# One Trainium2 core, a hybrid S5 and short-convolution layer with sixteen experts: everything up to the experts in a hand order

## The chip, the cores and the metric

The kernel runs on one core of one Trainium2 chip. The metric is the device time of one execution in microseconds (us), the median of the runs. The engines are TensorE (PE; its weight loads are PEld), VectorE (DVE), ScalarE (ACT), GpSimd (POOL) and SyncE (SP); SP issues most transfers, and each engine works through its own list in order.

## What is computed

x is (512, 1024), ctx (256, 1024), all in fp32. The reference, cut to what matters:

```python
mx = ada_mod(c, w_mod, b_mod)              # six vectors of 1024: silu(c) @ w_mod + b_mod
hx = modulate(x, norm1_g, mx[0], mx[1])    # rmsnorm(x, g) * (1 + scale) + shift
hc = modulate(ctx, norm1_g, mc[0], mc[1])  # mc: the same of c_ctx
zx = hx @ w_in                             # 256 columns for the S5 part, 3 x 768 for the convolution
y_s5 = s5_readout(...)                     # two diagonal complex scans, forward and backward, then GELU and a gate
y_conv = short_conv_latent(zx[..., 256:], conv_w)   # b * conv3(c * v), along rows and along columns
x = x + mx[2] * (concat(y_s5, y_conv) @ w_out)
h = modulate(x, norm2_g, mx[3], mx[4])     # routing: best of 4 groups, best 2 of its 4 experts
x = x + mx[5] * hier_moe(h, ...)           # 16 experts: (silu(h @ w1) * (h @ w3)) @ w2
return rmsnorm(x, final_g)
```

## The kernel before

Large products run in a split form: `split` (L75) writes an operand as a high part (a copy on ACT, L74) and a low part (a subtraction on DVE), and `mm3` (L97) multiplies high by high, low by high and high by low, so eight chunks of 128 make 24 matmuls of 128x512. Small products are plain fp32 (`mm`, L91), transposes L195.

The stages, in the order of the program:

- Modulation, first part: the first 2048 columns of w_mod come in 16 loads of 512 KB, [128, 8, 128] with runs of 512 B (L124, `load_mod`), each used by eight matmuls of 2 output rows (L91, 128*2). x and ctx come in, get normed row by row (L501 to L503, the Newton steps of `rsqrt` on DVE in L203 to L213), are transposed and scaled.
- u, the input projection of the S5 part (48 matmuls for x, 48 of half width for ctx).
- Tables of the S5 part: powers, input and output matrices, phasors W. Their complex products (`cmul`, L310 to L315: six elementwise instructions each) run on DVE (`MinT`, 128x1024) and on POOL (W, and the output matrices CA, 128x576).
- 18 conv blocks, six times c, v and b, each of 24 matmuls with a 512 KB piece of w_in; beside them the drive (L91, 128*64 128x96: two column halves of PE in alternation), the inside products (128*32 128x128: one group of 32 columns), the scans (L638 to L667) and the other 4096 columns of w_mod (`mod_rows`). These are summed up per row chunk by DVE (L735), or by ACT (L739) with POOL (L740), and then spread over the partitions by a matmul with ones_f.
- w_out: 16 pieces of 12 matmuls. POOL multiplies each piece by mx2 (L869), then it is split.
- Routing: logits (L937), the norm's factor rs, the choice by one-hot tables, a one-hot gather of expert 0's tokens by matmuls (X0, with the tables OH), the slot table and the indices idx. The modulated rows go to DRAM (td), from where POOL's indirect transfers gather the tokens of experts 1 to 15 (L1024). `columns(e)` transposes them (L195).
- 16 experts of up to 96 tokens each. Their weights come in pieces of 512 KB through a ring of 34 buffers; from piece 34 on a load waits for the load six pieces earlier.

Up to the experts a scheduler orders the instructions of each engine; the generators' calls (`run(cv_, 1)`, `run(mods_, 2)`) only say in which order it sees them. The experts are in an order written by hand (`tc.manual_schedule`), with SP left to the scheduler.

## Time and profile before

| | us |
|---|---|
| median of 3 runs (684.26 to 691.06) | 684.47 |
| the profiled execution | 688.22 |
| its span (first to last instruction) | 686.5 |
| PE busy in the span | 595.4 |
| DVE busy | 538.8 |
| ACT busy | 357.0 |
| POOL busy | 276.5 |

The span is the time from the first to the last recorded instruction of the profiled execution; 1.7 us of the execution lie around it. Busy time is what an engine's instructions take; matmuls are pipelined, so a busy PE can still wait inside for its weights. The granted clock (PEclk) is the share of TensorE's full clock that the chip let it have. A releaser, written behind an arrow, is what ended an engine's idle time.

### The profile page before, as it was taken

To read this page: it belongs to the slowest core of one execution; us is meant where nothing else is said; L and a number is where in the kernel's file an instruction comes from. 1 tells how busy PE (TensorE), PEld (TensorE's weight loads), DVE (VectorE), ACT (ScalarE), POOL (GpSimd) and SP (SyncE) were. 2 spreads that over 40 slices of the span, in tenths; PEclk is the share of its full clock that TensorE was granted. 3 is DMA by queue.
4 is the path that set the end of the run, shared out by engine and by line. 5 is a ranking of instruction groups with operands and counts; after the bars stand their busy time and mean duration, and the time that the engine had idled before them with its cause. 6 is when DMAs were issued, how large, how long until landed. Compare 5 with 4: busy or idle time off the path is not lost.

```text
span 686.5 us, 9226 instructions
## 1 busy us (share of the span) xinstructions
PE 595.4 (87%) x3002; PEld 441.8 (64%) x3003; DVE 538.8 (78%) x813; ACT 357.0 (52%) x498; POOL 276.5 (40%) x233
## 2 busy tenths in 40 slices
PE   6776839899787798999979999999999999999970
...
PEclk9797788899898799998968999999999999999996
...
GB/s 185 217 258 222 2 31 42 201 219 214 154 169 209 134 244 178 224 238 191 354 275 273 326 363 355 362 364 366 365 366 363 365 360 359 359 352 374 133 146 125
DMA packets 111091, 172.26 MB, mean 251 GB/s; under 512 B 14219, under 2 KB 51431, under 8 KB 111039
## 3 DMA queue, kind: packets, MB, share of 16 engines
...
## 4 chain that ended last, share of the span: by engine, by line
DMA 32%; issue 24%; DVE 18%; PE 16%; SPq 3%; ACT 3%; POOL 3%; POOLq 0%; DVEq 0%; ACTq 0%
DMA b<-td,idx 12%; PE bank L97 10%; DMA b<-in_w_mod_dram 7%; PE bank L91 4%; DMA yd<-b,idx 4%; DVE b L75 4%; DMA b<-in_w_in_dram 2%; DVE b L735 2%; DMA b<-in_expert_w_dram 1%; SPq L120 1%; ACT b L74 1%; DMA b<-in_norm_g_dram 1%; PE bank L195 1%; DMA b<-in_ctx_dram 1%; DMA b<-yd 1%
## 5 line engine op out<-in xcount | busy, mean ns | idle before, releaser
L97 PE MATMUL bank<-b,b 128*96 128x512 f32 (+2 forms) x1872 | 458.9, 402 | 22.3 <-DVE b L75 10.8
L97 PEld LDWEIGHTS bank<-b,b 128*96 128x96 f32 (+1 forms) x1872 | 322.4, 177 | 136.7 <-DVE b L75 14.7
L75 DVE TENSOR_TENSOR b<-b,b 128x1024 fp32r<-128x1024 f32 (+2 forms) x249 | 291.3, 1214 | 48.4 <-ACT b L74 46.1
L74 ACT ACTIVATE b<-b 128x1024 fp32r<-128x1024 f32 (+3 forms) x254 | 240.4, 980 | 77.4 <-POOL b L869 23.8
L1024 POOL DMA_INDIRECT b<-td,idx x15 | 18.8, 1255 | 194.5 <-PE bank L195 141.3
L1029 POOL DMA_INDIRECT yd<-b,idx x15 | 69.0, 4600 | 39.1 <-DVE b L1123 38.7
L195 PE MATMUL bank<-ident,b 96*128 96x96 f32 (+4 forms) x343 | 48.6, 279 | 24.9 <-ACT b L503 10.4
L195 PEld LDWEIGHTS bank<-ident,b 96*128 96x128 f32 (+4 forms) x343 | 41.0, 156 | 36.4 <-ACT b L503 10.7
L735 DVE SCALAR_TENSOR_TENSOR b<-b,sc,b 128x512 f32<-128x512 f32 x36 | 32.4, 899 | 25.9 <-DMA b<-in_w_mod_dram 16.8
L740 POOL TENSOR_TENSOR b<-b,b 128x512 f32<-128x512 f32 x21 | 30.8, 1468 | 47.7 <-ACT b L739 36.5
L74 ACT ACTIVATE b<-bank 128x384 fp32r<-128x384 f32 x46 | 22.0, 479 | 37.6 <-PE bank L195 37.6
L91 PE MATMUL bank<-b,sc 128*2 128x128 f32 x256 | 35.2, 302 | 7.1 <-DMA b<-in_w_mod_dram 6.7
L91 PE MATMUL bank<-b,b 128*64 128x96 f32 (+5 forms) x320 | 35.6, 289 | 6.4 <-DVE b L465 5.0
L869 POOL TENSOR_TENSOR b<-b,b 128x512 f32<-128x512 f32 x16 | 22.6, 1416 | 45.5 <-DMA b<-in_w_out_dram 33.3
L91 PEld LDWEIGHTS bank<-b,b 128*64 128x64 f32 (+3 forms) x312 | 27.5, 150 | 14.8 <-POOL b L740 5.4
L739 ACT ACTIVATE b<-b,sc 128x512 f32<-128x512 f32 x21 | 15.2, 723 | 38.2 <-DMA b<-in_w_mod_dram 38.2
L91 PEld LDWEIGHTS bank<-b,sc 128*2 128x2 f32 x256 | 22.8, 93 | 18.2 <-DMA b<-in_w_mod_dram 9.0
L75 DVE TENSOR_TENSOR b<-bank,b 128x384 fp32r<-128x384 f32 x46 | 25.3, 551 | 4.0 <-ACT b L74 3.9
L1123 DVE SCALAR_TENSOR_TENSOR b<-bank,gate,b 96x512 f32<-96x512 f32 x32 | 22.5, 739 | 1.3 <-PE bank L97 1.3
L501 ACT ACTIVATE b<-b 128x1024 f32<-128x1024 f32 x6 | 6.3, 1054 | 31.0 <-DMA b<-in_x_dram 23.7
L310 POOL TENSOR_TENSOR b<-b 128x16 f32<-128x16 f32 (+4 forms) x12 | 5.5, 455 | 30.7 <-DVE Asc L252 29.8
L503 ACT ACTIVATE b<-b,ss 128x1024 f32<-128x1024 f32 x6 | 6.9, 1149 | 20.2 <-DVE ss L213 19.0
...
## 6 DMA issues: line engine op xcount, KB each, us to landing
b<-in_expert_w_dram SPq DMA_DIRECT2D x192, 512.0 KB
...
```

The lines of the kernel that those rows point to most:

```text
L74: S.activation(hi, x_, AF.Copy)
L75: return (e or V).tensor_sub(lo, x_, f32(hi))
L91: T.matmul(o, l, r, start=start, stop=stop)
L97: T.matmul(o, l, r, start=start and n == 0, stop=stop and n == 2)
L195: T.transpose(o, i, ident[0:n, 0:n])
L735: V.scalar_tensor_tensor(acc[q], m[:, kk], sc[:, k:k + 1], acc[q], op0=OP.mult, op1=OP.add)
L739: S.activation(m[:, kk], m[:, kk], AF.Copy, scale=sc[:, k:k + 1])
L740: P.tensor_add(acc2, acc2, m[:, kk])
L869: P.tensor_mul(wor[i], wor[i], mx2[h])
L1024: return P.indirect_dma_start(out=xg, out_offset=None, in_=td[:, :], in_offset=bass.IndirectOffsetOnAxis(ap=idx[:, e:e + 1], axis=0), boun ...
L1029: P.indirect_dma_start(out=yd[:, :], out_offset=bass.IndirectOffsetOnAxis(ap=ix, axis=0), in_=src, in_offset=None, bounds_check=639, oob_i ...
L1123: V.scalar_tensor_tensor(yt[:, r], yb[h][0:CAP], gate[:, e:e + 1], mx5[h][0:CAP], op0=OP.mult, op1=OP.mult)
```

## The change

Everything before the experts is put into the hand order too, SP's list included: one `tc.manual_schedule` around the whole program. The 18 conv blocks become a loop of steps: split the weights of block i + 1, multiply block i, one unit of `mod_rows`, evict block i - 1, at most one piece of the S5 part for PE (`task`), and so much DVE work of the S5 part as fits a share of 5.0, 3.0 or 4.5 us by costs that the generators state (`spend`).

Beside the order the change alters work:

- w_mod's first part comes as [2, 512] pieces with runs of 2 KB, multiplied by 32 matmuls of 32 output columns by 512 in four column groups of PE, and a small matmul with `sel` adds the groups. B and C of the S5 part are loaded as they lie, in runs of 4 KB, and turned by PE.
- `mod_rows` is computed on PE: 16 units of four matmuls 32x512 in four column groups, a bias matmul ahead of every second, and `sel` in place of ones_f. Its sums on DVE, ACT and POOL go.
- The S5 tables W and CA are computed on DVE instead of POOL, in the loop.
- w_out: the first half is multiplied by mx2 after the product, the second half on DVE instead of POOL; six buffers; the S5 blocks come last.
- Routing: XA = XR * A2 on POOL; X0 is gathered from XR, scaled afterwards; the td rows, gates, tables, slots and counts come later, and gather(1) follows the slots beside expert 0; 40 instead of 22 warm-up matmuls.
- w1 and w3 pieces are loaded with runs of 4 KB (four rows to a partition), and the chunks of the tokens are taken with a stride of four (`chunk`). Loads wait for the one six earlier from piece 22 on; 20 pieces are requested before the td stores.

The diff, cut to its core:

```diff
+    order_ = tc.manual_schedule(engines={mybir.EngineType.PE, mybir.EngineType.DVE, mybir.EngineType.Activation,
+                                         mybir.EngineType.Pool, mybir.EngineType.SP})
+    order_.__enter__()
...
     def load_mod(q):
-        m = (q // 4 % 2) * 8 + q // 8 * 4 + q % 4
-        D.dma_start(wm_slot[q % 8], dap(w_mod, m * 128, [[6144, 128], [6144 * 128, 8], [1, 128]]))
+
+        D.dma_start(wm_slot[q % 8], dap(w_mod, q % 8 * 128 * 6144 + q // 8 * 512, [[6144, 128], [1024, 2], [1, 512]]))
...
+    def mod_pair(half, kp):
+
+        if kp == 0:
+            mb[:] = [nb("v"), nb("v")]
         for s in range(2):
...
-            cmul(P, W[:, 0, :, n + 1:n + m], W[:, 1, :, n + 1:n + m],
...
+            cmul(V, W[:, 0, :, n:n + m], W[:, 1, :, n:n + m], W[:, 0, :, 1:m + 1], W[:, 1, :, 1:m + 1],
...
+    def row_unit(u):
+
+        q, k4 = u // 2, u % 2
+        if k4 == 0:
+            rowb[0] = nb("m")
+            mm(rowb[0][0:32], ones_f[0:1, 0:32], acc[q][0:1], True, False)
+        for k in range(4 * k4, 4 * k4 + 4):
+            mm(rowb[0][group(k)], sc[:, k:k + 1].to_broadcast([128, 32]), mslot[k // 2 % 2][:, k % 2], 0 < k < 4, k >= 4)
+        row_loads(u + 1)
+
...
+        b = nb("m")
+        mm(b, sel[:, 0:1].to_broadcast([128, 128]), acc[q], True, True)
...
-                    if kk == 0 or q == 7:
-                        V.scalar_tensor_tensor(acc[q], m[:, kk], sc[:, k:k + 1], acc[q], op0=OP.mult, op1=OP.add)
-                    elif k2 == 0:
-                        S.activation(acc2, m[:, kk], AF.Copy, scale=sc[:, k:k + 1])
-                    else:
-                        S.activation(m[:, kk], m[:, kk], AF.Copy, scale=sc[:, k:k + 1])
-                        P.tensor_add(acc2, acc2, m[:, kk])
...
-            mm(b, ones_f, acc[q], True, True)
...
+        for u in range(16):
+            if u % 2 == 0 and u:
+                row_wide(u // 2 - 1)
+            row_unit(u)
+            if u % 2:
+                row_sum(u // 2)
+            yield
+        row_wide(7)
+        yield
...
+        return slice(q // 4 * 512 + q % 4, q // 4 * 512 + 512, 4)
...
-    w13 = [[(src[0, e, k2 * 256:(k2 + 1) * 256].rearrange("(k p) f -> p k f", p=128), [2, 512])
-            for src in (expert_w1, expert_w3) for k2 in range(4)] for e in range(16)] + [[]]
+    w13 = [[(src[0, e, k2 // 2 * 512:(k2 // 2 + 1) * 512].rearrange("(p j) f -> p j f", j=4)
+             [:, k2 % 2 * 2:k2 % 2 * 2 + 2], [2, 512]) for src in (expert_w1, expert_w3) for k2 in range(4)] for e in range(16)] + [[]]
...
-            if n_load[0] >= len(ring):
+            if n_load[0] >= 22:
                 after(d, loads[n_load[0] - 6], "few loads in flight")
...
+        if h == 1:
+            V.tensor_mul(wor[i], wor[i], mx2[h])
+        split(wor[i], woh[i], wol[i])
...
+    beside = in_turn(marked("in0", s5_input(0)), marked("in1", s5_input(1)), s5_phasors(), s5_output(0),
+                     marked("bb0", s5_inside(0)), s5_output(1), marked("bb1", s5_inside(1)),
+                     s5_scan(0), marked("scan", s5_scan(1)))
+
+    def spend(us):
+        while us > 0:
+            c_ = next(beside, None)
+            if c_ is None:
+                return
+            us -= c_
+
+    tasks = [("in0", lambda: s5_input_turned(0)), ("in1", lambda: s5_input_turned(1)),
+             (None, lambda: s5_drive(0)), (None, lambda: s5_drive(1)),
+             ("bb0", lambda: s5_inside_mm(0)), ("bb1", lambda: s5_inside_mm(1)),
+             ("scan", lambda: (s5_rows(0), s5_rows(1))), (None, s5_gelu), (None, s5_gelu_turned), (None, s5_glu)]
+
+    def task(ready):
+        if tasks and (tasks[0][0] is None or tasks[0][0] in ready):
...
+    for i in range(1, 18):
+        ready = set(done)
+        block_split(i + 1)
+        block_mm(i)
+        run(mods_, 1)
+        block_out(i - 1)
+        if len(tasks) > 4:
+            task(ready)
+        spend((5.0, 3.0, 4.5)[(i - 1) % 3])
...
-        V.tensor_mul(XA[i], XR[i], accp[2])
-    load_to(25)
-
-
-    with tc.issue_after(lg_mm[0].ins):
-        for _ in range(22):
-            mm(bank[3][:, 0:256], ones_b, ones_f.bitcast(BF), True, True)
+        P.tensor_mul(XA[i], XR[i], accp[2])
+    load_to(19)
...
-            mm(X0[k // 4][:, k % 4 * CAP:(k % 4 + 1) * CAP], XA[i][:, k * 128:(k + 1) * 128], OH0[i], i == 0, i == 3)
+            mm(X0[k // 4][:, k % 4 * CAP:(k % 4 + 1) * CAP], XR[i][:, chunk(k)], OH0[i], i == 0, i == 3)
...
-        V.scalar_tensor_tensor(XR[i], XA[i], rs[:, i:i + 1], accp[1], op0=OP.mult, op1=OP.add)
-        D.dma_start(td[i * 128:(i + 1) * 128, :], XR[i])
...
+        V.scalar_tensor_tensor(XA[i], XA[i], rs[:, i:i + 1], accp[1], op0=OP.mult, op1=OP.add)
+        D.dma_start(td[i * 128:(i + 1) * 128, :], XA[i])
+
+    first_parts(0)
+    gates(0)
+    first_parts(1)
+    gates(1)
+    ab = tables()
...
-    gather(1)
     load_to(len(ring) - 1)
...
+        slots(*ab)
+        gather(1)
+        counts()
```

**PE in the conv loop.** Before: the end of one block (L97; banks 63 to 70 are PSUM banks, b_... buffers), the wide sum of a row chunk over ones_f, and the drive.

```order
L97 MATMUL bank_65<-b_512_62_551,b_1024_93_638 128x512
L97 MATMUL bank_65<-b_512_54_543,b_1024_93_638 128x512
L97 MATMUL bank_65<-b_512_62_551,b_1024_90_635 128x512
L97 MATMUL bank_63<-b_512_56_545,b_1024_91_636 128x512
L91 MATMUL bank_67<-b_1024_6_77,ones_f 128x512
L91 MATMUL bank_68<-b_2560_110_988,b_4096_34_336 64x96 x8
L91 MATMUL bank_69<-b_2560_110_988,b_4096_34_336 64x96 x8
L97 MATMUL bank_63<-b_512_48_537,b_1024_91_636 128x512
```

After, between two blocks: the wide sum over `sel` (bank_70), the bias row (bank_67), four thin matmuls on the two row buffers, then the next block.

```order
L97 MATMUL bank_64<-b_512_57_209,b_1024_95_595 128x512
L97 MATMUL bank_64<-b_512_65_217,b_1024_92_592 128x512
L91 MATMUL bank_70<-b_1024_7_80,sel 128x512
L91 MATMUL bank_67<-b_1024_7_80,ones_f 32x512
L91 MATMUL bank_67<-b_1024_14_87,sc 32x512 x2
L91 MATMUL bank_67<-b_1024_15_88,sc 32x512 x2
L97 MATMUL bank_65<-b_512_58_210,b_1024_96_596 128x512
L97 MATMUL bank_65<-b_512_50_202,b_1024_96_596 128x512
```

What moved: four or five thin fp32 matmuls now stand between every two blocks, and a block's 24 matmuls are never interrupted.

**DVE and POOL before the conv blocks.** Before, on DVE: the S5 input table (L310 to L315, 128x1024) between the norm's one-column steps (L208, L212) and the last splits of u's operands (L75).

```order
L310 TENSOR_TENSOR b_1024_96_826<-b_288_31_333,b_512_32_334 128x1024
L208 SCALAR_TENSOR_TENSOR ss_471<-ss_471 128x1
L311 TENSOR_TENSOR b_1024_97_827<-b_288_31_333,b_512_32_334 128x1024
L75 TENSOR_TENSOR b_512_54_543<-b_512_46_535,b_512_62_551 128x512
L212 SCALAR_TENSOR_TENSOR ss_471<-ss_471 128x1
L312 TENSOR_TENSOR b_4096_95_825<-b_1024_96_826,b_1024_97_827 128x1024
L208 SCALAR_TENSOR_TENSOR ss_471<-ss_471 128x1
L313 TENSOR_TENSOR b_1024_96_826<-b_288_31_333,b_512_32_334 128x1024
```

Before, on POOL at the same time: the output table (128x576).

```order
L310 TENSOR_TENSOR b_576_100_954<-b_288_31_333,b_512_18_90 128x576
L311 TENSOR_TENSOR b_576_101_955<-b_288_31_333,b_512_18_90 128x576
L312 TENSOR_TENSOR b_4608_35_337<-b_576_100_954,b_576_101_955 128x576
L313 TENSOR_TENSOR b_576_100_954<-b_288_31_333,b_512_18_90 128x576
L314 TENSOR_TENSOR b_576_101_955<-b_288_31_333,b_512_18_90 128x576
L315 TENSOR_TENSOR b_4608_35_337<-b_576_100_954,b_576_101_955 128x576
```

After, the output table stands on DVE inside the loop (L432 to L439), between the weight split of a later block (L75, 128x1024), the convolution's sums of the block before (L720 to L735) and the next split.

```order
L75 TENSOR_TENSOR b_1024_91_591<-b_1024_8_81,b_1024_94_594 128x1024
L720 TENSOR_TENSOR b_640_108_737<-b_640_108_737,bank_64 128x512
L726 SCALAR_TENSOR_TENSOR b_512_102_731<-b_640_108_737,vT,b_512_102_731 128x512
L727 SCALAR_TENSOR_TENSOR b_512_102_731<-b_640_108_737,vT,b_512_102_731 128x512
L432 TENSOR_TENSOR b_576_156_1251<-b_288_40_186,b_512_44_190 128x576
L433 TENSOR_TENSOR b_576_157_1252<-b_288_40_186,b_512_44_190 128x576
L435 TENSOR_TENSOR b_4608_43_189<-b_576_156_1251,b_576_157_1252 128x576
L436 TENSOR_TENSOR b_576_156_1251<-b_288_40_186,b_512_44_190 128x576
L438 TENSOR_TENSOR b_576_157_1252<-b_288_40_186,b_512_44_190 128x576
L439 TENSOR_TENSOR b_4608_43_189<-b_576_156_1251,b_576_157_1252 128x576
L75 TENSOR_TENSOR b_1024_92_592<-b_1024_9_82,b_1024_95_595 128x1024
L735 TENSOR_TENSOR b_512_102_731<-b_512_102_731,bank_65 128x512
```

What moved: POOL has no table work left, the norms no longer share DVE with the tables, and six products of a table lie between two weight splits.

**DVE in the routing.** Before: the norm's factor (L213), the td rows (L1176, 128x1024), and between them the first step of the logits (L966, L967).

```order
L212 SCALAR_TENSOR_TENSOR rs<-rst,rs 128x4
L213 TENSOR_SCALAR rs<-rs 128x4
L1176 SCALAR_TENSOR_TENSOR b_1024_123_1987<-b_1024_127_1991,rs,b_1024_7_78 128x1024
L1176 SCALAR_TENSOR_TENSOR b_1024_124_1988<-b_1024_128_1992,rs,b_1024_7_78 128x1024
L1176 SCALAR_TENSOR_TENSOR b_1024_125_1989<-b_1024_129_1993,rs,b_1024_7_78 128x1024
L966 TENSOR_TENSOR lg<-bank_69,rs 128x80
L1176 SCALAR_TENSOR_TENSOR b_1024_126_1990<-b_1024_130_1994,rs,b_1024_7_78 128x1024
L967 TENSOR_TENSOR lg<-lg,crow 128x80
```

After: the last one-hot table (L1228), the td rows (L1414) behind it, and the first expert's split.

```order
L1228 TENSOR_SCALAR OH_2503<-slotI,RM,rs 128x96
L1414 SCALAR_TENSOR_TENSOR b_1024_122_780<-b_1024_122_780,rs,b_1024_7_80 128x1024
L1414 SCALAR_TENSOR_TENSOR b_1024_123_781<-b_1024_123_781,rs,b_1024_7_80 128x1024
L1414 SCALAR_TENSOR_TENSOR b_1024_124_782<-b_1024_124_782,rs,b_1024_7_80 128x1024
L1414 SCALAR_TENSOR_TENSOR b_1024_125_783<-b_1024_125_783,rs,b_1024_7_80 128x1024
L75 TENSOR_TENSOR b_768_191_2555<-b_768_189_2549,b_768_190_2554 128x384
```

After, further on: the two large tables (128x768), three splits of weight pieces, then the slots' copy, the gates and the indices (L1332).

```order
L1314 TENSOR_TENSOR b_384_192_2586<-slotI,rk 128x768
L1316 TENSOR_TENSOR b_384_193_2587<-OF,Dt 128x768
L75 TENSOR_TENSOR b_1024_202_2617<-b_1024_162_2035,b_1024_201_2616 128x1024
L75 TENSOR_TENSOR b_1024_204_2628<-b_1024_163_2037,b_1024_203_2627 128x1024
L75 TENSOR_TENSOR b_1024_205_2638<-b_1024_164_2039,b_1024_174_2254 128x1024
L1326 COPY b_96_206_2655<-bank_68 96x96
L1327 TENSOR_TENSOR gate<-b_96_206_2655 96x16
L1328 TENSOR_TENSOR gate<-gate,b_96_206_2655 96x16
L1330 SCALAR_TENSOR_TENSOR idf<-b_96_206_2655 96x16
L1331 TENSOR_SCALAR b_96_206_2655<-b_96_206_2655,dumpF 96x16
L1332 TENSOR_TENSOR idx<-idf,b_96_206_2655 96x16
```

What moved: the td rows from ahead of the logits to behind the one-hot tables, and the indices of the gathers behind the tables and three weight splits.

## Rows read from the trace of the kernel before

**Rows 1.** The page's forty slices of the span: PE's busy tenths, its granted clock.
```profile
PE   6776839899787798999979999999999999999970
...
PEclk9797788899898799998968999999999999999996
```

**Rows 2.** Stretches; columns: us, busy (x instructions) per engine, PEclk, DMA share, GB/s.
```profile
core 0: us, PE busy (x) PEld busy (x) DVE busy (x) ACT busy (x) POOL busy (x), PEclk, DMA share, GB/s
0.00:60.00 60.00, 41.06 (x293) 27.30 (x294) 25.59 (x201) 12.99 (x20) 24.34 (x81) 0.91 1.00 216
40.00:60.00 20.00, 14.54 (x126) 10.34 (x126) 7.70 (x43) 4.97 (x7) 15.49 (x49) 0.98 1.08 232
80.00:100.00 20.00, 10.58 (x51) 8.29 (x49) 20.00 (x16) 1.20 (x2) 19.47 (x10) 0.92 0.09 26
120.00:340.00 220.00, 193.26 (x986) 150.50 (x985) 149.32 (x160) 86.27 (x142) 104.16 (x82) 0.92 0.74 209
400.00:640.00 240.00, 239.98 (x1143) 170.54 (x1142) 231.69 (x249) 186.88 (x219) 81.02 (x26) 1.00 1.04 361
```

**Rows 3.** PE in order of time, 60 to 110 us; columns: start us, us, instruction, idle before.
```profile
61.40 4.31 PE L195 MATMUL bank<-ident,b 128*128 128x128 f32 x16 [0.96 <-ACT b L518]
66.91 1.22 PE L97 MATMUL bank<-b,b 128*128 128x512 f32 x2 [1.20 <-ACT b L74]
...
102.39 5.24 PE L195 MATMUL bank<-ident,b 128*128 128x128 f32 x26 [10.43 <-ACT b L503]
107.39 0.71 PE L97 MATMUL bank<-b,b 128*128 128x512 f32 x2
```

**Rows 4.** Groups, 79 to 103 us: busy us, mean ns | idle before, releaser.
```profile
L311 POOL TENSOR_TENSOR b<-b,b 128x576 f32<-128x576 f32 x2 | 4.4, 2210 | 0.0
...
L212 DVE SCALAR_TENSOR_TENSOR ss<-ss 128x1 f32<-128x1 f32 x3 | 4.1, 1357 | 0.0
...
L310 DVE TENSOR_TENSOR b<-b,b 128x1024 f32<-128x1024 f32 x2 | 3.5, 1744 | 0.0
...
L503 ACT ACTIVATE b<-b,ss 128x1024 f32<-128x1024 f32 x1 | 1.1, 1148 | 12.6 <-DVE ss L213 12.6
```

**Rows 5.** Groups, 120 to 340 us.
```profile
L97 PE MATMUL bank<-b,b 128*128 128x512 f32 x569 | 150.3, 420 | 15.2 <-ACT b L74 9.0 <-DVE b L75 6.1 <-POOL b L75 0.2
...
L735 DVE SCALAR_TENSOR_TENSOR b<-b,sc,b 128x512 f32<-128x512 f32 x36 | 32.4, 899 | 25.9 <-DMA b<-in_w_mod_dram 16.8 <-DMA b<-in_b_mod_dram 8.9
L740 POOL TENSOR_TENSOR b<-b,b 128x512 f32<-128x512 f32 x21 | 30.8, 1468 | 47.7 <-ACT b L739 36.5 <-DMA b<-in_x_dram 7.1 <-DVE b L735 4.0
...
L739 ACT ACTIVATE b<-b,sc 128x512 f32<-128x512 f32 x20 | 14.5, 723 | 38.2 <-DMA b<-in_w_mod_dram 38.2
...
L91 PE MATMUL bank<-b,ones_f 128*128 128x512 f32 x16 | 8.7, 623 | 4.3 <-POOL b L742 3.5 <-issue 0.8
```

**Rows 6.** PE in order of time, 139 to 169 us.
```profile
141.12 0.88 PE L91 MATMUL bank<-b,b 128*64 128x96 f32 x16 [0.18 <-ACT b L616]
...
165.06 3.68 PE L91 MATMUL bank<-b,b 128*32 128x128 f32 x32
```

**Rows 7.** PE in order of time, 336 to 386 us.
```profile
335.65 6.29 PE L97 MATMUL bank<-b,b 128*128 128x512 f32 x27
...
361.24 9.80 PE L91 MATMUL bank<-OH,b 128*128 128x96 f32 x64 [0.57 <-DVE OH L1009]
...
372.12 11.13 PE L97 MATMUL bank<-b,b 128*96 128x512 f32 x47 [0.46 <-DVE b L1058]
383.09 0.82 PE L195 MATMUL bank<-ident,b 96*128 96x96 f32 x8
```

**Rows 8.** DVE in order of time, 342 to 384 us.
```profile
342.96 1.22 DVE L954 TENSOR_TENSOR b<-b,b 128x1024 f32<-128x1024 f32 x1
...
349.95 0.16 DVE L212 SCALAR_TENSOR_TENSOR rs<-rst,rs 128x4 f32<-128x4 f32 x1
...
351.54 3.68 DVE L1176 SCALAR_TENSOR_TENSOR b<-b,rs,b 128x1024 f32<-128x1024 f32 x3
```

**Rows 9.** POOL in order of time, 374 to 384 us.
```profile
374.39 1.07 POOL L1024 DMA_INDIRECT b<-td,idx  x1 [41.38 <-ACT b L74]
```

1026 lines of the change are left out of this document (572 added, 454 removed).

## The prediction

> **What bounds the kernel now.** I read the page's forty slices first, then a table of stretches, then TensorE in order of time at the places that it pointed to. The slices show two kernels in one [rows 1]: from the 22nd slice (360 us) on PE stands at 9, and before that it has holes, the deepest a 3 in the sixth slice (86 to 103 us), with the granted clock at 0.7 to 0.9 around it. The stretches say why [rows 2]. From 400 to 640 us PE is busy 239.98 of 240 us while the DMA engines are full at 361 GB/s: the experts are bound by PE, with the loads close behind, and the change does little inside them. In the first 60 us the DMA engines are as full but move only 216 GB/s (13.0 MB in all), 232 in the last 20 of them at a share of 1.08. From 80 to 100 us nothing is loaded (26 GB/s), PE works 10.6 us, and DVE and POOL are busy without a break with 16 and 10 instructions. From 120 to 340 us PE is busy 193.3 of 220 us: 26.7 us idle, at a clock of 0.92.
>
> So the work divides by TensorE's milestones in the program [rows 3, 7]: the input projection u starts at 66.9 us, the conv blocks at 107.4, w_out ends at 341.9, expert 0 starts at 372.1, and expert 1's columns come at 383.1. From there 303 us follow that I leave as they are, wider weight runs included: PE has no idle time there for them to take away. All of it is worked in the profiled execution's time (688.22 us, 3.75 above the median of the runs); I carry the difference over to the median of 684.47.
>
> **Up to the conv blocks (107.4 us now).** The same 13 MB are loaded, but w_mod's runs grow from 512 B to 2 KB and the parameters B and C come in 4 KB runs. The stretch that carries 2 KB runs and more moves 361 GB/s [rows 2], the one with the short runs 232. I take 340, nearer to the row with the same run length: 13.0 / 0.340 = 38 us, and 3 us until the first byte: 41 us. Behind the last piece stand its matmuls, an eviction, eight small matmuls, two adds, and four scalings with their splits, some 6.5 us, so u starts at 47.5 (66.9 now). Its 48 matmuls take 11.5 us at 0.24 (27 in 6.29 us [rows 7], so 0.233, and a little for the clock), the 16 transposes of ctx 4.3 [rows 3], block 0 another 24 x 0.24 = 5.8, ctx's 48 half-width matmuls 5.8: 74.9, and 3 us of waits: the loop's first matmul at 78. That is 29.4 us earlier. Two causes carry it: 19.4 us are the loads, and the rest is the hole. There DVE and POOL share the S5 tables, and each stretches the other [rows 4]: a 128x1024 product takes 1.74 us on DVE (1.22 where POOL is still [rows 8]), a 128x576 one 2.21 on POOL, and the norm's one-column instructions 1.36 where 128x4 ones take 0.16 elsewhere [rows 8]. ACT waits 12.6 us for that norm, and PE waits for ACT 10.4 [rows 3, 4]. With the tables moved into the loop and off POOL, that wait has no cause left. Ends: 73 (361 GB/s, no waits) and 93 (232 GB/s: 56 us of loads).
>
> **Conv blocks to the end of w_out (234.5 us now: 107.4 to 341.9).** Block 0 leaves: -5.8. The 32 transposes of the S5 inputs, before the blocks now (26 of them in 5.24 us at a low clock [rows 3]), come into it: +4.1 at the pace of 8 in 1.03 us. The second part of the modulation leaves DVE (36 x 0.90 = 32.4 us), ACT (21 x 0.72) and POOL (21 x 1.47) [rows 5] and becomes 64 thin fp32 matmuls, 32 output columns by 512, on PE, the engine that bounds; the eight wide sums stay (16 records, 8.7 us [rows 5]). Price of one unit of four: the trace has no such unit. What it has is one column group used again and again, 32 records of 128 columns in 3.68 us, so 115 ns each, and two column groups in alternation, 16 records of 96 columns in 0.88 us, so 55 ns where one group would need 86 [rows 6]; without the first record's start the pair is close to twice as fast. A unit is eight records of 512 columns: one after another 8 x 0.46 = 3.68 us, two side by side 1.84, all four side by side 0.92. I take 1.84, the row that is nearest in kind: 16 x 1.84 = +29.4. The bias matmul ahead of every second unit shares that unit's first group, so it stands alone: 8 x 2 x 0.46 = +7.4.
>
> [...] The pair in this trace gains 86 / 55 = 1.56, start included; no run here has three or four groups. [...]
>
> What the block order gives back: DVE loses those 32 us and POOL's disturbance and gains the tables. Counted by form at the durations that such forms have alone (splits 17 x 1.2, block outputs 6 x 2.7, tables 12 x 1.22, 24 x 0.75 and 14 us of smaller ones, scans 30, the rest 4), its share of the loop is some 117 us, an estimate: 6.9 per step against 5.8 + 1.8 + 1 to 2 on PE. PE no longer waits for splits that queue behind long DVE work, since a split now stands a whole step ahead of its matmuls. Of 26.7 us idle I leave 5 (the row loads have only two slots, so a load of some 4 to 6 us must land within one step; one gelu chain): -21.7. The conv and w_out matmuls take 150.3 / 569 = 0.264 us here [rows 5] where I count 0.24: with the holes closed I give half of that back, 569 x 0.024 / 2 = -6.8. POOL's products for w_out go: hidden by the loads now, nothing. Sum: 234.5 - 5.8 + 4.1 + 29.4 + 7.4 - 21.7 - 6.8 = 241.1. So w_out ends at 78 + 241.1 = 319.1 (341.9 now): 22.8 us gained, all of it from the first part.
>
> **From w_out to expert 1's columns (41.2 us now).** Four products leave DVE (1.22 each) and four row updates of 1.28 that stood ahead of the logits go behind the one-hot tables [rows 8]; 40 warm-ups instead of 22 are hidden. POOL takes the four products at 2.3 us or so, and DVE's two-operand instructions of the norm wait beside them as in [rows 4]: +4.7. The gather matmuls then start 15.5 us after w_out (19.3 now) and take 9.8 [rows 7]. But the tables, the slots and the gather of expert 1 now come after them: tables until about +32, three weight splits of 1.2 us queued ahead of the slots' copy on DVE, the gather's issue at +37, and 8.7 us from there to the columns as now (374.4 [rows 9] to 383.1 [rows 7]). That is +45.7 where it is 41.2 now: 4.5 us given back, since PE has only 11 us of expert 0 to do meanwhile, from +27. Ends: nothing (the gather's 7 us land under expert 0) and 10.
>
> Sum: 22.8 - 4.5 = 18.3 us off: 669.9 for the profiled execution, 666.2 for the median.
>
> **Rivals.** (1) The four column groups run one after another. What speaks for it: fp32 records of one group in a row do just that [rows 6], and no row has four groups. Against: two groups clearly overlap. Price 16 x (3.68 - 1.84) = 29.4 us on the bounding engine: 695, slower than before; it decides from 3.4 us a unit on. (2) DVE sets the loop's steps: its order is fixed now, so a table piece that runs over its share holds back the next split. Against: 6.9 of about 9 us a step. One us more in each of 17 steps is 17 us: 683, no change to be told. (3) The experts run dry: 20 weight pieces instead of 30 are requested before expert 0, and the loads there have hardly any reserve (DMA share 1.04 [rows 2]). Price up to 10 us: 676. (4) All four groups side by side and the loads at 361 GB/s: -14.7 and -5: 646.
>
> **How the numbers follow.** Forecast 0.50; (4) 0.20; (2) 0.13; (1) 0.09; (3) 0.08. A measurement of this kernel can tell about 1% (6.8 us) from no change. Faster by more: forecast, (3) and (4), 0.78; within: (2), 0.13; slower: (1), 0.09. The forecast's own range is 650 to 678 (the loads' ends and what idle time is left). The range for 8 in 10 runs from 643 (below (4)) to 690 (above (2)); it leaves out (1) and little else.
>
> **What would show it.** Right: u's first matmul near 47 us and no hole of 10 us after it; the loop's step near 9 us, with PE idle under 1 us a step; a thin unit near 1.8 us; w_out's end near 319; gather(1) issued some 37 us after it, with PE waiting for the columns about 7 us; experts as before. Wrong: a unit near 3.7 or 0.9; first u after 60; DVE as releaser of most of PE's idle time in the loop; PE waiting for expert weights after 400.

## The result and the profile after

The changed kernel takes 678.33 us (median of 20 runs, 675.93 to 683.91) where the kernel before takes 686.06 beside it (20 runs): a ratio of 0.9894, 95% interval 0.9867 to 0.9921. It is faster, by 7.3 us, where 18.3 were forecast; one run of before, at 717.3 us, lay in a slower state and is left out of the ratio, from which the 7.3 us come (the medians lie 7.7 apart). The profiled execution took 677.51 us, its span 675.8; against the 686.5 of before that is 10.7 us, and in this difference the accounts below are made (before's profiled execution lay 2.2 us above its median here, after's 0.8 below).

TensorE's milestones, in us from the start of the span:

| | before | forecast | after |
|---|---|---|---|
| u's first matmul | 66.9 | 47.5 | 52.95 |
| conv blocks begin (after: block 1) | 107.4 | 78 | 78.8 |
| from there to the end of w_out | 234.5 | 241.1 | 235.1 |
| end of w_out | 341.9 | 319.1 | 313.9 |
| from there to expert 1's columns | 41.15 | 45.7 | 53.62 |
| from there to the end of the span | 303.37 | 303.4 | 308.22 |

So 28.0 us are gained up to the end of w_out, more than was forecast, and 12.47 + 4.85 = 17.3 are given back behind it, where 4.5 were.

The page's slices after, in answer to [rows 1]:

```profile
PE   4779979999989998999795999999999999999980
PEclk9688999999989999799767999999999999999985
```

The 3 in the sixth slice is gone. What is left of a hole stands in slices 20 to 22 (321 to 372 us), a 7, a 9 and a 5, with the clock at 0.7, 0.6 and 0.7: between w_out and the first columns.

The stretches, in answer to [rows 2] (100 to 320 us is now the larger part of the conv loop, and w_out):

```profile
core 0: us, PE busy (x) PEld busy (x) DVE busy (x) ACT busy (x) POOL busy (x), PEclk, DMA share, GB/s
0.00:60.00 60.00, 40.05 (x219) 24.24 (x221) 37.89 (x179) 28.76 (x42) 7.09 (x25) 0.83 0.91 252
100.00:320.00 220.00, 212.75 (x1165) 155.22 (x1164) 144.64 (x219) 74.86 (x135) 23.07 (x31) 0.97 0.58 178
332.00:348.00 16.00, 15.10 (x62) 14.35 (x62) 6.98 (x16) 4.56 (x10) 0.00 (x0) 0.50 0.92 344
366.00:374.00 8.00, 5.88 (x20) 4.19 (x21) 2.25 (x3) 2.85 (x5) 1.01 (x1) 0.50 1.03 378
400.00:640.00 240.00, 240.00 (x1129) 172.61 (x1128) 227.92 (x243) 182.64 (x213) 59.59 (x25) 1.00 0.95 340
```

From 100 to 320 us PE idles 7.25 us of 220 (26.7 before, from 120 to 340), and the experts are still bound by PE, now with room on the DMA engines (0.95 against 1.04). In two stretches PE runs at half clock: 332 to 348, although it is busy 15.1 of 16 us there, and 366 to 374.

PE in order of time at the milestones, in answer to [rows 3, 6, 7]:

```profile
51.15 1.95 PE L91 MATMUL bank<-sel,b 128*128 128x2 f32 x16 [2.39 <-DVE b L258]
52.95 12.78 PE L97 MATMUL bank<-b,b 128*128 128x512 f32 x48
...
67.29 11.97 PE L97 MATMUL bank<-b,b 128*128 128x512 f32 x74
...
109.77 1.06 PE L91 MATMUL bank<-b,sc 128*32 128x512 f32 x8
110.77 5.73 PE L97 MATMUL bank<-b,b 128*128 128x512 f32 x24
116.43 1.61 PE L91 MATMUL bank<-b,sc 128*32 128x512 f32 x8
...
308.17 5.75 PE L97 MATMUL bank<-b,b 128*128 128x512 f32 x24
...
330.51 15.25 PE L91 MATMUL bank<-OH,b 128*128 128x96 f32 x64 [0.68 <-DVE OH L1228]
...
367.54 2.20 PE L198 MATMUL bank<-ident,b 96*128 96x96 f32 x12 [7.16 <-DMA b<-td,idx]
...
401.51 1.08 PE L198 MATMUL bank<-ident,b 96*128 96x96 f32 x8
```

u follows the modulation's small sums without the tables' hole; the row of 74 is ctx's 48, block 0's 24 and the first two of block 1, so block 1 begins at 67.29 + 11.97 less two matmuls, 78.8. A thin unit of eight records takes 1.06 us, and 1.61 where it stands directly behind a block. The last row of w_out ends at 313.92. X0 takes 15.25 us where it took 9.80, and before the first columns PE waits 7.16 us for gather(1). The last row is eight transposes of an expert's columns in the steady run of the experts: 1.08 us.

The groups, in answer to [rows 5]: the sums of the second part of the modulation, L735 on DVE, L739 on ACT and L740 on POOL in the kernel before, are gone, and in their place stand the thin matmuls and the bias rows.

```profile
L91 PE MATMUL bank<-b,sc 128*32 128x512 f32 x128 | 21.3, 627 | 6.2 <-DMA b<-in_w_mod_dram 6.2
...
L91 PE MATMUL bank<-b,ones_f 1*32 1x512 f32 x16 | 8.3, 600 | 0.0
```

DVE behind w_out, in answer to [rows 8]:

```profile
316.00 0.47 DVE L1182 TENSOR_TENSOR ss<-ss 128x4 f32<-128x4 f32 x1
316.50 4.58 DVE L206 TENSOR_SCALAR rst<-ss 128x4 f32<-128x4 f32 x3
321.00 0.16 DVE L207 TENSOR_SCALAR rs<-rst 128x4 int32<-128x4 int32 x1
321.19 2.23 DVE L208 TENSOR_SCALAR rs<-rs 128x4 int32<-128x4 int32 x1
323.45 0.16 DVE L213 TENSOR_TENSOR rst<-rs 128x4 f32<-128x4 f32 x1
...
345.79 1.24 DVE L1276 TENSOR_SCALAR b<-bank,AST 128x96 f32<-128x96 f32 x4 [3.10 <-PE bank L91]
...
352.41 3.49 DVE L75 TENSOR_TENSOR b<-b,b 128x1024 fp32r<-128x1024 f32 x3
...
356.85 0.18 DVE L1332 TENSOR_TENSOR idx<-idf,b 96x16 int32<-96x16 f32 x1
```

POOL in the same stretch, in answer to [rows 9]:

```profile
314.06 9.29 POOL L1174 TENSOR_TENSOR b<-b,b 128x1024 f32<-128x1024 f32 x4 [81.21 <-DVE b L1124]
...
358.01 1.61 POOL L1242 DMA_INDIRECT b<-td,idx  x1 [34.62 <-DMA b<-in_expert_w_dram]
```

Read the two together. The norm's first steps are 128x4, and two of them (4.58 us for three) and L208 each take about as long as one of POOL's four products that run beside them; with POOL's end at 323.35 DVE is back to 0.16. Then X0's eviction (L1276) waits on DVE until PE has finished X0, and behind it in DVE's list come the rest of the gates, the tables and the indices (L1332), so gather(1) is issued at 358.01, 44.1 us after w_out.

### The profile page after: what moved, and what is told of

Its sections match the earlier page's. It is cut to its first block, busy times and chain, and to the rows that moved or that the text cites. A ratio compares the mean times of both kernels' runs of the same rounds, so it can differ in the third digit from the quotient of the medians.

```text
span 675.8 us, 9072 instructions
## 1 busy us (share of the span) xinstructions
PE 611.0 (90%) x3048; PEld 439.0 (65%) x3049; DVE 512.1 (76%) x836; ACT 349.2 (52%) x488; POOL 113.0 (17%) x103
## 4 chain that ended last, share of the span: by engine, by line
PE 76%; DMA 11%; DVE 5%; ACT 3%; SPq 2%; issue 1%; POOL 0%; POOLq 0%; DVEq 0%; ACTq 0%
PE bank L97 59%; PE bank L91 12%; DMA b<-in_w_mod_dram 6%; PE bank L198 4%; DMA b<-td,idx 1%; DMA b<-in_s_b_re_dram 1%; DMA b<-in_expert_w_dram 1%; SPq L164 1%; DMA b<-in_ctx_dram 1%; DVE rst L206 1%; ACT b L680 1%; DVE b L75 1%; DMA b<-yd 1%; DVE b L1492 0%; ACT b L1463 0%
## 5 line engine op out<-in xcount | busy, mean ns | idle before, releaser
L97 PE MATMUL bank<-b,b 128*96 128x512 f32 (+2 forms) x1872 | 449.4, 397 | 2.4 <-DVE b L1276 0.9
L97 PEld LDWEIGHTS bank<-b,b 128*96 128x96 f32 (+1 forms) x1872 | 319.1, 175 | 117.9 <-issue 7.5
L75 DVE TENSOR_TENSOR b<-b,b 128x1024 fp32r<-128x1024 f32 (+2 forms) x246 | 268.1, 1136 | 41.3 <-ACT b L74 40.8
L74 ACT ACTIVATE b<-b 128x1024 fp32r<-128x1024 f32 (+2 forms) x246 | 234.3, 990 | 49.8 <-DVE b L992 22.3
L198 PE MATMUL bank<-ident,b 96*128 96x96 f32 (+3 forms) x323 | 46.6, 286 | 26.1 <-DMA b<-td,idx 7.2
L198 PEld LDWEIGHTS bank<-ident,b 96*128 96x128 f32 (+3 forms) x323 | 43.2, 186 | 36.2 <-issue 8.3
L1247 POOL DMA_INDIRECT yd<-b,idx x15 | 51.2, 3412 | 41.7 <-DVE b L1403 41.4
L91 PE MATMUL bank<-b,b 128*64 128x96 f32 (+7 forms) x384 | 50.8, 372 | 0.3
L75 DVE TENSOR_TENSOR b<-bank,b 128x384 fp32r<-128x384 f32 x46 | 25.4, 553 | 12.4 <-ACT b L74 12.4
L91 PE MATMUL bank<-b,sc 128*32 128x512 f32 x128 | 21.3, 627 | 6.2 <-DMA b<-in_w_mod_dram 6.2
L91 PE MATMUL bank<-OH,b 128*128 128x96 f32 x64 | 15.2, 439 | 0.7 <-DVE OH L1228 0.7
L91 PEld LDWEIGHTS bank<-OH,b 128*128 128x128 f32 x64 | 15.0, 330 | 0.8 <-DVE OH L1228 0.8
L91 PEld LDWEIGHTS bank<-b,sc 128*32 128x32 f32 x128 | 3.1, 108 | 18.3 <-DMA b<-in_w_mod_dram 9.5
L1274 ACT ACTIVATE b<-bank,AST 128x96 f32<-128x96 f32 x4 | 1.4, 429 | 21.7 <-PE bank L91 21.7
```

The lines of the kernel that those rows point to most:

```text
L74: S.activation(hi, x_, AF.Copy)
L75: return (e or V).tensor_sub(lo, x_, f32(hi))
L91: T.matmul(o, l, r, start=start, stop=stop)
L97: T.matmul(o, l, r, start=start and n == 0, stop=stop and n == 2)
L198: T.transpose(o, i, ident[0:n, 0:n])
L1247: P.indirect_dma_start(out=yd[:, :], out_offset=bass.IndirectOffsetOnAxis(ap=ix, axis=0), in_=src, in_offset=None, bounds_check=639, oob_i ...
```

## The experiments

Each starts from the changed kernel. Ratios are to the kernel before, timed beside it; differences in us are between medians and the 678.33 of after; the kernel before, timed beside each, had medians from 684.99 to 686.27, so about 1 us of such a difference means nothing. The end of w_out is not a fixed point: in the profiled executions of e1, e2, e3, e6, e9 and e10, which alter next to nothing ahead of it, it lay between 310.9 and 317.7 (after: 313.9). Stretches behind it are therefore counted from it.

### e1_plain_rows: w1, w3 and the tokens' chunks as before

```diff
-        return slice(q // 4 * 512 + q % 4, q // 4 * 512 + 512, 4)
+        return slice(q * 128, (q + 1) * 128)
...
-    w13 = [[(src[0, e, k2 // 2 * 512:(k2 // 2 + 1) * 512].rearrange("(p j) f -> p j f", j=4)
+    w13 = [[(src[0, e, k2 * 256:(k2 + 1) * 256].rearrange("(k p) f -> p k f", p=128), [2, 512])
```

> The expert weights, the router weights and the chunks of the tokens are taken as in the kernel before (runs of 2 KB, chunks of 128 columns side by side); all else as after the change. Theory (strided weights on PE): the change made PE load weights with a stride of four elements in X0 and in the columns of every expert. The eight transposes of an expert then stand 0.08 us apart again instead of 0.12, so the period of an expert falls from 17.92 to 17.65 us (14 x 0.27 = 3.8 us), X0's records from 0.233 to 0.21 us at half clock, some 1.5 us, or 15.3 to 10 us if the clock comes up in it as it did before: 5 to 9 us faster than after the change, about 670 us. Rival (the period grew because the loads are late, or for the clock): the period stays at 17.9 or grows, since shorter runs load more slowly, and the time stays at 678 or rises.

The edit also gives the loads their runs of 2 KB back; e9 and e10 part the two.

Measured: 669.23 us, ratio 0.9767 (0.9735 to 0.9798), 9.1 us less than after. PE in order of time:

```profile
330.22 10.23 PE L91 MATMUL bank<-OH,b 128*128 128x96 f32 x64 [0.68 <-DVE OH L1223]
...
361.36 2.18 PE L198 MATMUL bank<-ident,b 96*128 96x96 f32 x12 [5.67 <-DMA b<-td,idx]
...
413.59 0.82 PE L198 MATMUL bank<-ident,b 96*128 96x96 f32 x8
```

X0 is back to 10.23 us, and all that follows it on DVE comes forward with it: the columns stand 47.7 us behind w_out instead of 53.6. Eight transposes of an expert's columns take 0.82 us where after takes 1.08, and the period of an expert is 17.72 us, as before (17.96 after; means of 13). One edit that I had not priced at all costs more than the whole change gains. The clock in X0:

```profile
330.00:336.00 6.00, 5.78 (x27) 5.78 (x28) 5.67 (x8) 0.00 (x0) 0.00 (x0) 0.50 0.52 207
336.00:340.00 4.00, 4.00 (x37) 4.00 (x37) 0.65 (x2) 3.03 (x6) 0.00 (x0) 0.97 0.96 346
```

It starts at half clock here too, but recovers after 6 us.

### e2_xa_on_dve: XA = XR * A2 back on DVE, behind the tables

```diff
-    for i in range(4):
-        P.tensor_mul(XA[i], XR[i], accp[2])
...
     for i in range(4):
+        V.tensor_mul(XA[i], XR[i], accp[2])
         V.scalar_tensor_tensor(XA[i], XA[i], rs[:, i:i + 1], accp[1], op0=OP.mult, op1=OP.add)
```

> The product of the rows with A2 is moved from POOL, where it runs beside the norm's factor, to DVE behind the one-hot tables, ahead of each row's update. Theory (POOL holds up DVE): the first five instructions of the norm's factor took 7.4 us beside POOL's four products (three of them 2.2 to 2.3 us each) and take 0.8 when POOL is still; X0 starts 6 to 7 us earlier after the end of w_out (10 instead of 16.6). If the gather of expert 1 still comes from the indices, it comes earlier by the same 6 us, and the time is about 672. Rival (the clock or the gather sets the end): the gap before X0 goes, but X0 at half clock and the wait for the gather take it up, and the time stays within 2 us of 678.

Measured: 672.88 us, ratio 0.9824 (0.9805 to 0.9842), 5.5 us less than after. The norm on DVE:

```profile
319.85 0.31 DVE L206 TENSOR_SCALAR rst<-ss 128x4 f32<-128x4 f32 x3
...
320.26 0.17 DVE L208 TENSOR_SCALAR rs<-rs 128x4 int32<-128x4 int32 x1
```

Without POOL's products the same four instructions take 0.5 us instead of 6.8, X0 starts 10.6 us after w_out instead of 16.6, and the columns come 46.5 after it. X0 itself, though, still takes 15.25 us, and here PE came to it without a gap, but for the 0.68 us that it waits for OH in every one of these runs:

```profile
322.83 4.53 PE L91 MATMUL bank<-ones_f,ones_b 128*128 128x256 bf16 x40
...
328.20 15.25 PE L91 MATMUL bank<-OH,b 128*128 128x96 f32 x64 [0.68 <-DVE OH L1226]
```

```profile
328.00:331.00 3.00, 2.80 (x12) 2.80 (x13) 2.96 (x6) 0.00 (x0) 0.00 (x0) 1.00 1.03 408
...
335.00:339.00 4.00, 4.00 (x19) 4.00 (x19) 3.96 (x4) 2.93 (x6) 0.00 (x0) 0.50 0.56 224
```

So neither the gap nor the clock is what makes X0 long. Its first records run at full clock and follow each other by 2.80 / 12 = 0.23 us; later the granted clock is at 0.50, with PE busy without a break, and the pace is 4.00 / 19 = 0.21. Over the 64 it is 0.24. In X0 a record with strided chunks takes this long at either clock.

### e3_slots_first: tables, slots and gather(1) ahead of expert 0's splits

```diff
-    first_parts(0)
     gates(0)
-    first_parts(1)
     gates(1)
     ab = tables()
+    first_parts(0)
+    first_parts(1)
+    slots(*ab)
+    gather(1)
+    counts()
...
-        slots(*ab)
-        gather(1)
-        counts()
```

> Gates, tables, slots, counts and the gather of expert 1 are put ahead of expert 0's first operands on DVE and ACT, and ahead of expert 0's matmuls on PE. Theory (the gather is late by its place in the order): the gather is issued near 348 us instead of 358, expert 1's columns come without the 7.2 us of PE idle time, and the clock does not fall to half behind it: 7 to 10 us faster than after the change, about 670 us. Rival (it is late because of td's stores or the queue's loads): the gather is issued earlier but lands no earlier than 364, and expert 0 starts later by the work put ahead of it: within 3 us of 678.

Measured: 669.74 us, ratio 0.9782 (0.9759 to 0.9805), 8.6 us less than after.

```profile
331.53 15.25 PE L91 MATMUL bank<-OH,b 128*128 128x96 f32 x64 [0.68 <-DVE OH L1228]
...
361.23 1.53 PE L198 MATMUL bank<-ident,b 96*128 96x96 f32 x12 [0.47 <-DMA b<-td,idx]
```

X0 is as slow as in after, and the slots' matmuls still stand behind it on PE, but gather(1) is now issued at 351.31, 4.5 us after X0's end instead of 12.3, PE waits 0.47 us for it instead of 7.16, and the first columns follow at full clock (1.00 from 352 us on). The tables and splits that stood between X0 and the slots made that wait, not the transfer.

### e4_one_group: the thin matmuls in one column group

```diff
-            mm(rowb[0][group(k)], sc[:, k:k + 1].to_broadcast([128, 32]), mslot[k // 2 % 2][:, k % 2], 0 < k < 4, k >= 4)
+            mm(rowb[0][0:32], sc[:, k:k + 1].to_broadcast([128, 32]), mslot[k // 2 % 2][:, k % 2], False, k == 7)
```

The wide sum's `sel` becomes a column of `ident`, so that it takes that group alone.

> The thin matmuls of the second part of the modulation all write the first group of 32 columns instead of four groups; the wide sum takes that group alone. Theory (the four groups run side by side: the trace after shows four matmuls in 1.05 us): in one group a unit takes 8 x 0.43 to 0.46 = 3.4 to 3.7 us, 16 units cost 16 x 2.5 = 40 us more on PE in the loop, which is bound by PE: 36 to 42 us slower than after the change, 715 to 720 us. Rival (the loop has slack, or the groups do not matter): under 15 us slower.

Measured: 707.97 us, ratio 1.0335 (1.0314 to 1.0355), 29.6 us more than after; the end of w_out 32.0 later.

```profile
110.70 3.62 PE L91 MATMUL bank<-b,sc 128*32 128x512 f32 x8
```

A unit in one group takes 3.62 us, the 3.68 that I had worked out from [rows 6]; the 128 records are busy 57.9 us where they are 21.3 in four groups. Of the 36.6 us between, 6.2 are the units' waits for w_mod, which vanish beside slower units; that leaves 30.4. My expectation took every unit at 1.06 and no wait away, hence too much. Rival (1), the groups one after another, is excluded for after; had it come, the kernel would have been slower than before, as that rival said.

### e5_short_runs: w_mod's first part in runs of 512 B

```diff
-        D.dma_start(wm_slot[q % 8], dap(w_mod, q % 8 * 128 * 6144 + q // 8 * 512, [[6144, 128], [1024, 2], [1, 512]]))
+        for c_ in range(4):
+            D.dma_start(wm_slot[q % 8][:, :, c_ * 128:(c_ + 1) * 128],
+                        dap(w_mod, q % 8 * 128 * 6144 + q // 8 * 512 + c_ * 128, [[6144, 128], [1024, 2], [1, 128]]))
```

> The 16 loads of w_mod's first part are cut into four each of 128 columns, so that every run is 512 B again as in the kernel before; matmuls and order stay. Theory (the run length sets the pace of the first 50 us): the first 60 us move some 215 to 235 GB/s instead of 252, u's first matmul comes 5 to 10 us later than 53.0, and the whole is 5 to 10 us slower than after the change (683 to 688 us). Rival (not the length of the runs but what stood between the loads, the norms and DVE's order, made u late before): u within 2 us of 53.0, time within 3 us of 678. Four times as many transfers also cost SP four times the issues, some 0.33 us each, 16 us more in 45: this may add to the delay.

Measured: 691.58 us, ratio 1.0082 (1.0055 to 1.0108), 13.3 us more than after, more than expected.

```profile
0.00:60.00 60.00, 42.80 (x198) 22.87 (x199) 31.28 (x161) 22.62 (x33) 5.46 (x23) 0.80 0.90 212
```

The rate falls to 212 GB/s, near before's 216 [rows 2], with the DMA engines as busy as in after (0.90 and 0.91), and u starts at 58.55. So at most 5.6 of the 14 us by which u comes earlier are the runs of w_mod; the other 8.4 lie in the order and in B and C, which I did not part. The edit makes four transfers of one, so it also lengthens SP's list (an issue of such a load takes 0.37 us in after, the last of the 16 is out by 36.6, and in e5 PE still waits for w_mod until 54.93), and PE's waits for w_mod grow from 6.2 to 13.4 us. Run length and number of transfers are not parted here, so the run length alone is worth 13 us at the most.

### e7_tables_on_pool: W and CA back on POOL, in the loop

```diff
-            cmul(V, W[:, 0, :, n:n + m], W[:, 1, :, n:n + m], W[:, 0, :, 1:m + 1], W[:, 1, :, 1:m + 1],
+            cmul(P, W[:, 0, :, n:n + m], W[:, 1, :, n:n + m], W[:, 0, :, 1:m + 1], W[:, 1, :, 1:m + 1],
...
-            yield from cmul_steps(CA[:, d, 0, gl], CA[:, d, 1, gl], pw[0], pw[1], cv_[0], cv_[1], ct1, ct2, 1.4)
+            yield from cmul_pool(CA[:, d, 0, gl], CA[:, d, 1, gl], pw[0], pw[1], cv_[0], cv_[1], ct1, ct2, 1.4)
```

> The phasors W and the output tables of the S5 part are computed on POOL again, in the places that the hand order gives them; the input tables stay on DVE. Theory (PE bounds the loop and its splits stand a step ahead, so that DVE's slack hides what POOL does to it): PE's idle time in the loop grows by under 3 us, time within 4 us of 678. Rival (sharing between DVE and POOL was what made the hole before the conv blocks, wherever it stands): splits of 1.2 us take 2 us and more, PE waits for them in most steps, and the time rises by 8 us or more.

Measured: 698.23 us, ratio 1.0168 (1.0109 to 1.0228), 19.9 us more than after; my theory fell. The largest piece, on PE, POOL and DVE:

```profile
166.64 8.00 PE L97 MATMUL bank<-b,b 128*128 128x512 f32 x22 [11.42 <-DVE b L75]
```

```profile
146.21 3.53 POOL L770 MEMSET b<- 128x4096 f32 x1 [10.01 <-PE bank L91]
```

```profile
157.43 0.45 DVE L513 TENSOR_SCALAR kd<-jk 32x16 f32<-32x16 int32 x1 [17.64 <-POOL jk L512]
...
164.15 4.55 DVE L75 TENSOR_TENSOR b<-b,b 128x1024 fp32r<-128x1024 f32 x2
```

PE waits 11.42 us for a split on DVE, and DVE stood 17.64 us waiting for a small index table that lies in POOL's list behind a clearing (which itself waited 10.01 us for PE) and six products. In the main that is a queue. But the engines also stretch each other here: the splits behind it take 4.55 us for two beside POOL's products, where one takes 1.22 in after. PE then pays again: the 22 matmuls behind the wait take 8.00 us, where e8's take 5.29, and the granted clock is 0.74 over 154 to 180 us.

### e8_pool_not_in_the_way: e7 with the index table early and the clearing on DVE

```diff
+    P.iota(jk, pattern=[[1, 16]], base=16, channel_multiplier=-1)
...
-            P.iota(jk, pattern=[[1, 16]], base=16, channel_multiplier=-1)
...
-        P.memset(bbd[d], 0.0)
+        V.memset(bbd[d], 0.0)
```

> As the run with the tables on POOL, but the index row jk is made at the start of the program, and DVE clears the inside matrices itself, so that no DVE instruction waits for one that stands behind the tables in POOL's list. Theory (in that run the loss was a queue: DVE stood 17.6 us before jk, behind two output tables and a clearing that itself waited 10 us for the drive; a weight split stood behind it on DVE, and PE waited 11.4 us for the split): PE's wait of 11.4 us and the half clock after it (2.7 us) go, 682 to 686 us. Rival (DVE and POOL slow each other down, wherever the tables stand): splits still come late by their own length, PE's waits for DVE stay above 8 us, and the time is 692 or more.

Measured: 689.68 us (683.08 to 690.02), ratio 1.0016 (0.9983 to 1.0049), 8.6 us less than e7 and 11.4 more than after. In the profiled executions w_out ends at 318.5 (e7 333.0, after 313.9), and PE's longest wait for a split is 2.5 us. The median lies between the theory's 686 and the rival's 692; the waits are the theory's. So the queue was 14.5 of e7's 19.1 us by the profiles, 8.6 of 19.9 by the medians; the profiled execution is the fastest of e8's nine. What is left of the price of tables on POOL, 5 to 11 us with the clearings on DVE, is not settled further.

### e6_all_three: e1, e2 and e3 together

The edits of e1, e2 and e3, nothing else; of each its core:

```diff
-        return slice(q // 4 * 512 + q % 4, q // 4 * 512 + 512, 4)
+        return slice(q * 128, (q + 1) * 128)
...
-        P.tensor_mul(XA[i], XR[i], accp[2])
...
+        V.tensor_mul(XA[i], XR[i], accp[2])
...
     ab = tables()
+    first_parts(0)
+    first_parts(1)
+    slots(*ab)
+    gather(1)
```

> Plain rows, the product with A2 on DVE behind the one-hot tables, and slots and gather ahead of expert 0, together. Theory (three waits in a row on one chain): X0 starts about 10.5 us after w_out's end, takes 10 us, the gather is issued some 25 us after it and lands under expert 0, the clock stays up, and an expert takes 17.65 us: 678.3 - 9.1 - 5.5 - 8.6, of which the wait for the gather (5.7 us left with plain rows) is counted twice in part: 656 to 661 us, 24 to 28 us faster than the kernel before. Rival (the loads become the bound, since PE now asks for the pieces 25 us earlier): PE waits for expert weights from 400 us on, and the time is 664 or more.

Measured: 660.84 us, ratio 0.9657 (0.9584 to 0.973): 17.5 us less than after and the fastest of all versions.

```profile
323.04 7.43 PE L91 MATMUL bank<-OH,b 128*128 128x96 f32 x64 [0.68 <-DVE OH L1221]
339.48 0.80 PE L91 MATMUL bank<-b,b 128*96 128x96 bf16 x8 [9.00 <-DVE b L1309]
...
353.36 0.82 PE L198 MATMUL bank<-ident,b 96*128 96x96 f32 x8
```

```profile
323.00:330.00 7.00, 6.96 (x62) 6.96 (x62) 6.89 (x9) 0.00 (x0) 0.00 (x0) 1.00 0.70 266
```

X0 takes 7.43 us at full clock, and the columns come 42.4 us behind w_out. The three gains do not add up there (5.9 + 7.2 + 7.4 us alone, 11.2 together), since all three shorten the same way to gather(1); once it lands in time, PE waits 9.00 us for the tables instead.

### e9_stride_two and e10_stride_two_all: a stride of two, with the runs of 4 KB kept

A partition takes two whole rows of w1 or w3 instead of four halves of a piece, so a run is 4 KB still, and the chunks' elements lie 8 bytes apart instead of 16.

```diff
-        return slice(q // 4 * 512 + q % 4, q // 4 * 512 + 512, 4)
+        return slice(q // 2 * 256 + q % 2, q // 2 * 256 + 256, 2)
...
-    w13 = [[(src[0, e, k2 // 2 * 512:(k2 // 2 + 1) * 512].rearrange("(p j) f -> p j f", j=4)
+    w13 = [[(src[0, e, k2 * 256:(k2 + 1) * 256].rearrange("(p j) f -> p j f", j=2), [2, 512])
```

e9 is after with this edit, e10 is e6 with it in the place of plain chunks. If it is the distance between the elements that costs, X0 comes near e1's 10.23 us in e9; if any stride costs alike, it stays at 15.25.

> The chunks of the tokens, and the weights' rows with them, with a stride of two instead of four; w1 and w3 keep their runs of 4 KB. [...] Rival: any stride costs as stride four does: X0 15.25, transposes 1.08, period 17.97, 678 us. [...]

> The same stride of two, with XA's products back on DVE behind the tables and the slots ahead of expert 0's splits (e2 and e3). Theory: as e6, X0 7.4 us at full clock and about 661 us, with the long runs kept; should the long runs be worth anything where the experts are bound by PE, a little under e6. Rival: X0 stays at 15.25 us; its excess of 7.8 us is then only partly hidden, since the slots' matmuls stand behind X0 on PE, but PE waits 9 us for the tables there anyway: 663 to 667 us, with 3 us of them in the periods of 17.97.

Measured: e9 673.28 us, ratio 0.9844 (0.9796 to 0.9891), 5.1 us less than after; e10 667.05 us, ratio 0.9714 (0.9671 to 0.9758). PE of e9:

```profile
330.24 10.75 PE L91 MATMUL bank<-OH,b 128*128 128x96 f32 x64 [0.68 <-DVE OH L1227]
...
415.26 1.08 PE L198 MATMUL bank<-ident,b 96*128 96x96 f32 x8
```

and of e10:

```profile
329.94 7.79 PE L91 MATMUL bank<-OH,b 128*128 128x96 f32 x64 [0.68 <-DVE OH L1225]
```

Each of the two readings, that the distance costs and that any stride costs alike, is half right. In X0 a stride of two is nearly free (10.75 against 10.23 plain, 7.79 against 7.43), where four doubles the time (15.25 in e2 against 7.43 in e6), so there it is the distance that costs. In the columns' transposes a stride of two costs what four does (1.08, the period 17.94), so there both strides cost alike (e1, plain: 0.82 and 17.72). And in the sum the long runs bring nothing: behind w_out e10 takes 42.8 + 305.8 = 348.6 us, e6 42.4 + 305.5 = 347.9. Below that sum lie 2.6 us more in e10's 13 periods (233.27 against 230.68), those of the transposes, and 2.2 us less behind them (58.8 against 61.1); e6's PE waits 1.30 us for a split there and e10's does not, but whether the long runs spared it that was not tried. e10's median lies 6.2 us over e6's; in the two profiled executions 6.7 us are the way to w_out, which ended at 317.7 and 310.9, and the edit alters next to nothing there.

## Why the prediction was right or wrong

**What held.** The hole ahead of the conv blocks went, and the loop began at 78.8 (78). The loop stayed bound by PE, and a split on DVE holds PE up once in it, 0.9 us. Rivals (1) and (2) did not come: e4 shows what (1) would have cost, and (3) neither, for PE is busy 240.00 of 240 us in the experts. Of (4) the thin units came near (1.06 us beside its 0.92, where no block stands before them), the loads did not. PE waited for gather(1) for 7.16 us (7). What the hole owed to the tables' place, to POOL's share of them and to the order is not parted: no run put the tables back between u and the loop.

**Two terms that were off and made up for each other.** The loads to u: I took 340 GB/s, the first 60 us moved 252, and u came at 52.95 instead of 47.5. The answer of the DMA engines for these 60 us, in 40 slices of 1.5 us:

```profile
GB/s 0 145 367 252 79 52 56 116 166 279 313 259 238 225 160 388 240 191 250 202 217 384 377 388 391 386 382 391 388 329 293 276 190 226 169 195 309 268 186 358
```

The rate that I took is reached and passed (377 to 391, from 31.5 to 43.5 us), but from 6 to 31.5 us it lies at 52 to 313, with one slice of 388. The 3 us until the first byte were my estimate, and no run shows them: before's first bytes move between 1.5 and 1.8 us, after's too. The way from u to the loop took 25.9 us instead of 30.5 and gave 4.6 of the 5.5 us back: the 3 us of waits did not come, and ctx's transposes took 1.9 us, not 4.3. So that the loop began as forecast is in good part luck.

**Three terms of the loop.** The stretch from the loop's begin to the end of w_out, before and after:

```profile
107.40:341.90 234.50, 206.48 (x1066) 162.09 (x1064) 160.46 (x172) 93.39 (x161) 112.24 (x88) 0.93 0.71 202
```

```profile
78.80:313.90 235.10, 223.35 (x1179) 159.07 (x1179) 152.22 (x225) 75.88 (x134) 22.70 (x38) 0.97 0.59 177
```

The forecast's terms make 206.5 - 5.8 + 4.1 + 29.4 + 7.4 - 6.8 = 234.8 us of busy PE, and leave 28.0 - 21.7 = 6.3 idle. PE is busy 223.35. A thin unit takes 1.06 to 1.61 us, not 1.84: 21.3 us for all, with 8.3 for the bias rows, where 29.4 + 7.4 stood; that is 7.2 us less. The block matmuls take another 4 less: 600 in 147.1 us, so 0.245 each, where the forecast's 0.264 with half of 0.024 given back makes 0.252. The two are the 11.4 us of work less. The idle time is 11.75 us, 5.4 more than forecast; 6.2 of it are the thin units' waits for w_mod. Together the stretch is 6.0 us shorter than forecast; with a begin 0.8 later, w_out ends at 313.9 and not at 319.1. Four fp32 column groups gain 3.62 / 1.06 = 3.4 over one (e4), and 3.62 / 1.61 = 2.2 where the unit stands behind a block; the forecast's 1.84 took a gain of two.

**The step that failed: "The gather matmuls then start 15.5 us after w_out (19.3 now) and take 9.8", and with it "+45.7 where it is 41.2 now".** The start was nearly right (16.6). The 9.8 was not: the new chunks read the weights of these 64 matmuls with a stride of four, and I had no price for it. X0 took 15.25 us. The chain to gather(1) runs through X0, since its eviction stands on DVE ahead of the tables, so the excess passed on in full: 1.1 us later start, 5.45 in X0, 0.55 between, 0.8 in the transfer, together the 7.9 by which 53.6 exceeds 45.7. e1 shows the cause (10.23 us with plain chunks, the columns 5.9 earlier), and e9 that it is the stride and not the loads' runs (10.75 us with the runs of 4 KB kept). e3 shows the other half, the order: X0 at 15.25 us still, but the tables ahead of its eviction, and the columns come 7.4 earlier. That order stood in the forecast, with its tables until +32 and its issue at +37, but with X0 at 9.8.

That the start came near is in part luck. The terms that the step names make 19.3 - 4.9 - 5.1 + 4.7 = 14.0, not 15.5. And I gave the norm +4.7 for its two-operand instructions beside POOL's products; held up were in the main one-operand ones, three times about 2.3 us, and e2 shows that without POOL's products X0 starts at 10.6, so they cost 6.0. The 2.23 us of L208 are about one of POOL's products (9.29 us for four, so 2.3 each); how POOL holds DVE up, no run shows.

**The other failed step: "303 us follow that I leave as they are, wider weight runs included: PE has no idle time there for them to take away".** An engine without idle time can still be made slower, and it took 308.2. Of these 4.9 us, 3.1 lie in the 13 periods from expert 2's columns to expert 15's (233.43 us against 230.31), 0.24 each, and 2.3 in expert 1's own, which runs at half clock (0.50 from 366 to 374 us) behind the wait of 7.16 us; the end gives 0.5 back. The experiments part them crosswise: e1, with plain chunks and a wait of 5.67 us, has the 13 periods at 230.32 and expert 1's at +3.1; e3, strided and without the wait, has 233.38 and -0.1.

The 0.24 are the transposes of the columns, whose weights are the strided chunks: eight of them take 1.08 us at full clock (1.00 from 400 to 640 us), in e1 0.82, and 0.82 before as well [rows 7]. What the wider runs were to give, they did give to the DMA engines (from 400 to 640 us a share of 0.95 at 340 GB/s, where e6 with runs of 2 KB has 0.98 at 339), and those were not what bounds.

**The sum.** 28.02 - 12.47 - 4.85 = 10.7 us in the profiles, where 22.8 - 4.5 stood. With the strided chunks priced at what e1 shows, 9.1 us, the forecast would have been 675 by my own reckoning of the rest.
